# Binary cross entropy over two 8192 x 8192 matrices: chunks taken from the four quarters in turn, and the last chunk in four pieces

## The chip, the cores and the metric

One core of a Trainium2 chip. Times are device microseconds of one execution, medians of several runs. The granted clock was 1.0. A "span" is the profiled part of one execution, about 1.85 us shorter than its time.

## The reference

```python
# pred: uniform 0.01..0.99, target: 0 or 1; both (8192, 8192) float32
pred = np.clip(pred, 1e-7, 1 - 1e-7)
return -(target * np.log(pred) + (1 - target) * np.log(1 - pred))
```

Both inputs must be read and one output written: 3 x 268.4 MB = 805.3 MB. Since target is 0 or 1, the kernel takes one logarithm: -ln|pred + target - 1|.

## The kernel before

The matrices are flattened and cut into n = 64 chunks of 128 partitions x 8192. A ring of four slots holds pred as float32 (the result overwrites it) and target as bf16; the cast is done by the transfer. Chunk k's pred, target and result are 4.194 MB each in DRAM.

```python
def load(k):
    queue = nc.sync if k == 0 else nc.gpsimd
    queue.dma_start(out=slot(ring_p, k), in_=pred_c[k])
    nc.gpsimd.dma_start(out=slot(ring_t, k), in_=target_c[k])

def store(k, off=0, w=W):
    queue = nc.sync if k >= n - 2 else nc.gpsimd
    queue.dma_start(out=out_c[k, :, off : off + w], in_=slot(ring_p, k, off, w))

# clip(k):  DVE   p = min(max(p, eps), 1 - eps)      (L67)
# front(k): DVE   p = (t - 1) + p                    (L73)
#           ACT   p = Abs(p)                         (L76)
#           ACT   p = Ln(p)                          (L77)
# back(k):  DVE   p = -p                             (L81)
...
for k in range(1, n - 1):
    clip(k); front(k); back(k - 1); store(k - 1)
    if k >= 2 and k - 2 + SLOTS < n:
        load(k - 2 + SLOTS)
back(n - 2)
store(n - 2)

h, q = W // 2, W // 4              # the last chunk: 4096, 2048, 2048
clip(n - 1)
front(n - 1, 0, h)
front(n - 1, h, q)
back(n - 1, 0, h)
store(n - 1, 0, h)
front(n - 1, h + q, q)
back(n - 1, h, q)
back(n - 1, h + q, q)
store(n - 1, h, h)
```

(The four statements on one line stand on lines of their own in the kernel.)

## Time and profile before

| | before |
|---|---|
| time, median of 3 runs | 1871.18 us (1870.36 to 1873.4) |
| span of the profiled run | 1869.4 us |
| DVE, ACT busy | 60%, 48% of the span |
| DRAM traffic | 805.3 MB, 431 GB/s over the span |
| clip starts once settled | 29.04 to 29.05 us apart |

From the page of the kernel before: busy tenths of each engine in 40 equal slices of the span (9 is 90% or more), the mean of the 16 DMA engines, what they moved on the on-chip side (a target chunk counts half there, being cast to bf16), and the DRAM traffic.

```profile
DVE  4946564666656656566565665656656666566564
ACT  3643644536355364453544535445354463553645
DMA  9999999999999999999999999999999999999998
GB/s 325 337 377 352 351 376 344 376 353 350 381 344 373 358 347 385 344 368 364 346 384 346 361 370 344 382 350 355 375 345 378 353 351 381 345 372 358 347 385 330
HBM read 536.87 MB, written 268.44 MB: 431 GB/s over the span
```

The DMA row is full but for the last slice; no compute engine is. That is a kernel bound by transfers. How near to a ceiling it runs is read from the pace of a DVE instruction that waits for a load. From the timeline of the kernel before (start us, duration us, engine, line, operation, out<-in; in brackets the idle time before it and what ended it):

```profile
344.98 4.43 DVE L67 TENSOR_SCALAR ring_p<-ring_p 128x8192 f32<-128x8192 f32 x1 [6.26 <-DMA ring_p<-in_pred_dram]
375.27 4.43 DVE L67 TENSOR_SCALAR ring_p<-ring_p 128x8192 f32<-128x8192 f32 x1 [6.94 <-DMA ring_p<-in_pred_dram]
...
549.85 4.43 DVE L67 TENSOR_SCALAR ring_p<-ring_p 128x8192 f32<-128x8192 f32 x1 [6.31 <-DMA ring_p<-in_pred_dram]
578.89 4.43 DVE L67 TENSOR_SCALAR ring_p<-ring_p 128x8192 f32<-128x8192 f32 x1 [6.29 <-DMA ring_p<-in_pred_dram]
```

Early on two starts can be 30.29 us apart; later they are 29.04 us apart, one chunk for one chunk: 12.58 MB / 29.05 us = 433 GB/s. The trace also records every DMA packet: a 32 KB packet took 1213 ns at the median, and the 99th percentile was 1226 ns.

The tail, from the same timeline. "x3" on the SP line merges the last three stores: the third issue ends at 1836.16 + 26.10 = 1862.26.

```profile
1799.12 4.43 DVE L67 TENSOR_SCALAR ring_p<-ring_p 128x8192 f32<-128x8192 f32 x1 [6.25 <-DMA ring_p<-in_pred_dram]
1808.86 8.69 DVE L73 SCALAR_TENSOR_TENSOR ring_p<-ring_t,ring_p 128x8192 f32<-128x8192 bf16 x1 [5.31 <-DMA ring_t<-in_target_dram]
...
1831.70 4.43 DVE L81 TENSOR_SCALAR ring_p<-ring_p 128x8192 f32<-128x8192 f32 x1 [9.82 <-ACT ring_p L77]
1836.05 4.42 DVE L67 TENSOR_SCALAR ring_p<-ring_p 128x8192 f32<-128x8192 f32 x1
1836.16 26.10 SPq L63 DMA_DIRECT2D out_dram<-ring_p  x3
1840.50 6.63 DVE L73 SCALAR_TENSOR_TENSOR ring_p<-ring_t,ring_p 128x4096 f32<-128x4096 bf16 x2
...
1860.67 1.23 DVE L81 TENSOR_SCALAR ring_p<-ring_p 128x2048 f32<-128x2048 f32 x1 [2.78 <-ACT ring_p L77]
```

And the tail in windows of 2 us (start:end, length, busy time of DVE, ACT and POOL with instruction counts, granted clock, mean busy share of the 16 DMA engines, GB/s):

```profile
1850.00:1852.00 2.00, 0.00 (x0) 2.00 (x1) 0.00 (x0) 1.00 1.02 442
1852.00:1854.00 2.00, 1.74 (x1) 2.00 (x2) 0.00 (x0) 1.00 0.42 180
1854.00:1856.00 2.00, 2.00 (x2) 1.93 (x2) 0.00 (x0) 1.00 0.48 205
1856.00:1858.00 2.00, 1.89 (x2) 1.22 (x1) 0.00 (x0) 1.00 1.12 475
1858.00:1860.00 2.00, 0.00 (x0) 1.97 (x2) 0.00 (x0) 1.00 0.98 418
1860.00:1862.00 2.00, 1.23 (x1) 0.64 (x1) 0.00 (x0) 1.00 0.08 33
1862.00:1864.00 2.00, 0.00 (x0) 0.00 (x0) 0.00 (x0) 1.00 0.72 303
1864.00:1866.00 2.00, 0.00 (x0) 0.00 (x0) 0.00 (x0) 1.00 1.14 483
1866.00:1868.00 2.00, 0.00 (x0) 0.00 (x0) 0.00 (x0) 1.00 0.62 262
```

There are two holes, at 1852 to 1856 and 1860 to 1862.

### The profile page before, as it was taken

Reading aid. Unit: us, or ns where it says so; the run is one execution under the profiler, and the core shown is the slowest. Engines: PE = TensorE matmul, PEld = TensorE weight load, DVE = VectorE, ACT = ScalarE, POOL = GpSimd, SP = SyncE. Lnnn points to the kernel's source line nnn. Section 1 sums busy time; section 2 is a strip of 40 time slices with the busy share of each in tenths; the row PEclk is TensorE's granted clock in tenths of the full one; section 3 lists DMA queues with packets and bytes.
Section 4 is the critical chain, followed back from the end, with each engine's and each line's share of the span. In section 5 each row is a group of like instructions: output and inputs, shape, how many; then the busy total and the mean of one; then the engine's idle time right before and its main releaser. Section 6 shows DMA issues by size and latency. Waiting matters only on the chain.

```text
span 1869.4 us, 755 instructions
## 1 busy us (share of the span) xinstructions
DVE 1117.4 (60%) x197; ACT 902.2 (48%) x134; POOL 110.6 (6%) x193
## 2 busy tenths in 40 slices
DVE  4946564666656656566565665656656666566564
ACT  3643644536355364453544535445354463553645
POOL 0210000000000000000000000000000000000000
DMA  9999999999999999999999999999999999999998
GB/s 325 337 377 352 351 376 344 376 353 350 381 344 373 358 347 385 344 368 364 346 384 346 361 370 344 382 350 355 375 345 378 353 351 381 345 372 358 347 385 330
DMA packets 27797, 671.14 MB, mean 359 GB/s; under 512 B 3088, under 2 KB 3088, under 8 KB 3088
## 3 DMA queue, kind: packets, MB, share of 16 engines
q0 software_dynamic: 27216, 658.52, 98.8%
q1 hardware_dynamic: 576, 12.58, 1.6%
q14 instruction: 5, 0.04, 0.0%
HBM read 536.87 MB, written 268.44 MB: 431 GB/s over the span
## 4 chain that ended last, share of the span: by engine, by line
issue 86%; DMA 6%; POOL 5%; DVE 2%; ACT 1%; POOLq 0%; DVEq 0%; PEldq 0%
DMA ring_t<-in_target_dram 4%; DMA out_dram<-ring_p 2%; POOL ring_t L59 2%; POOL out_dram L63 2%; POOL ring_p L58 1%; DVE ring_p L73 1%; ACT ring_p L76 1%; ACT ring_p L77 1%; DVE ring_p L81 1%; DVE ring_p L67 0%; POOLq L58 0%; DVEq L73 0%; PEldq L136 0%; POOLq L63 0%
## 5 line engine op out<-in xcount | busy, mean ns | idle before, releaser
L76 ACT ACTIVATE ring_p<-ring_p 128x8192 f32<-128x8192 f32 (+1 forms) x66 | 450.4, 6824 | 955.6 <-DVE ring_p L73 955.6
L73 DVE SCALAR_TENSOR_TENSOR ring_p<-ring_t,ring_p 128x8192 f32<-128x8192 bf16 (+1 forms) x66 | 556.5, 8433 | 325.1 <-DMA ring_t<-in_target_dram 325.0
L67 DVE TENSOR_SCALAR ring_p<-ring_p 128x8192 f32<-128x8192 f32 x64 | 283.3, 4426 | 400.9 <-DMA ring_p<-in_pred_dram 400.9
L77 ACT ACTIVATE ring_p<-ring_p 128x8192 f32<-128x8192 f32 (+1 forms) x66 | 450.4, 6824 | 2.1
L81 DVE TENSOR_SCALAR ring_p<-ring_p 128x8192 f32<-128x8192 f32 (+1 forms) x66 | 283.1, 4290 | 17.7 <-ACT ring_p L77 17.7
L63 POOL DMA_DIRECT2D out_dram<-ring_p x62 | 40.8, 658 | 1692.7 <-DVE ring_p L81 1662.7
L58 POOL DMA_DIRECT2D ring_p<-in_pred_dram x63 | 36.1, 573 | 18.4 <-DMA out_dram<-ring_p 18.1
L59 POOL DMA_DIRECT2D ring_t<-in_target_dram x64 | 35.3, 552 | 0.8 <-PEq L136 0.8
L87 ACT ACT_TABLE_LOAD x1 | 1.3, 1283 | 0.7 <-PEq L125 0.7
L86 DVE MEMSET warm<- 1x8 f32 x1 | 0.1, 65 | 0.8 <-PEq L125 0.8
L87 ACT ACTIVATE warm<-warm 1x8 f32<-1x8 f32 x1 | 0.2, 207 | 0.0
L125 POOL MEMSET const-float32-0.0<- 128x1 f32 x1 | 0.1, 99 | 0.2 <-issue 0.2
L125 POOL MEMSET const-bfloat16-1.0<- 128x1 bf16 x1 | 0.1, 102 | 0.0
L125 POOL MEMSET const-float32-1.0<- 128x1 f32 x1 | 0.1, 99 | 0.0
L125 POOL MEMSET const-uint8-127<- 128x1 uint8 x1 | 0.1, 99 | 0.0
## 6 DMA issues: line engine op xcount, KB each, us to landing
ring_p<-in_pred_dram POOLq DMA_DIRECT2D x63, 4096.0 KB, 34.5
out_dram<-ring_p POOLq DMA_DIRECT2D x62, 4096.0 KB, 25.3
ring_t<-in_target_dram POOLq DMA_DIRECT2D x64, 2048.0 KB, 43.6
ring_p<-in_pred_dram SPq DMA_DIRECT2D x1, 4096.0 KB, 19.6
out_dram<-ring_p SPq DMA_DIRECT2D x1, 4096.0 KB, 21.1
out_dram<-ring_p SPq DMA_DIRECT2D x2, 2048.0 KB, 6.9
```

What stands on the lines that cost most here:

```text
L58: queue.dma_start(out=slot(ring_p, k), in_=pred_c[k])
L59: nc.gpsimd.dma_start(out=slot(ring_t, k), in_=target_c[k])
L63: queue.dma_start(out=out_c[k, :, off : off + w], in_=slot(ring_p, k, off, w))
L67: nc.vector.tensor_scalar(out=p, in0=p, scalar1=EPS, scalar2=1 - EPS, op0=Alu.max, op1=Alu.min)
L73: nc.vector.scalar_tensor_tensor(out=p, in0=t, scalar=1.0, in1=p, op0=Alu.subtract, op1=Alu.add)
L76: nc.scalar.activation(out=p, in_=p, func=Act.Abs)
L77: nc.scalar.activation(out=p, in_=p, func=Act.Ln)
L81: nc.vector.tensor_scalar(out=p, in0=p, scalar1=-1.0, scalar2=None, op0=Alu.mult)
L86: nc.vector.memset(warm, 1.0)
L87: nc.scalar.activation(out=warm, in_=warm, func=Act.Ln)
L125: nc = _bacc.Bacc("TRN2", target_bir_lowering=False, num_devices=1)
```

## The change: intent and diff

The order of chunks changes: each quarter of the matrices is 16 chunks, and the new walk visits quarters so that over the run every quarter's store comes behind a load of every other quarter. The sizes and the order of the transfers on their queues stay. In the tail, the last chunk's clip moves ahead of the multiply of the last but one, and its passes become four of 2048.

```diff
+QUARTERS = [0, 0, 1, 0, 2, 0, 3, 1, 1, 2, 1, 3, 2, 2, 3, 3]
+
+def walk(n):
+    taken, order = [0] * 4, []
+    assert n % 32 == 0
+    for i in range(n):
+        q = QUARTERS[i // 2 % 16]
+        order.append(q * (n // 4) + taken[q])
+        taken[q] += 1
...
-        queue.dma_start(out=slot(ring_p, k), in_=pred_c[k])
-        nc.gpsimd.dma_start(out=slot(ring_t, k), in_=target_c[k])
+        queue.dma_start(out=slot(ring_p, k), in_=pred_c[order[k]])
+        nc.gpsimd.dma_start(out=slot(ring_t, k), in_=target_c[order[k]])
...
-        queue.dma_start(out=out_c[k, :, off : off + w], in_=slot(ring_p, k, off, w))
+        queue.dma_start(out=out_c[order[k], :, off : off + w], in_=slot(ring_p, k, off, w))
...
+        clip(n - 1)
         back(n - 2)
         store(n - 2)
 
-        h, q = W // 2, W // 4
-        clip(n - 1)
-        front(n - 1, 0, h)
-        front(n - 1, h, q)
-        back(n - 1, 0, h)
-        store(n - 1, 0, h)
-        front(n - 1, h + q, q)
-        back(n - 1, h, q)
-        back(n - 1, h + q, q)
-        store(n - 1, h, h)
+        q = W // 4
+        front(n - 1, 0, q)
+        front(n - 1, q, q)
+        front(n - 1, 2 * q, q)
+        back(n - 1, 0, q)
+        back(n - 1, q, q)
+        store(n - 1, 0, 2 * q)
+        front(n - 1, 3 * q, q)
+        back(n - 1, 2 * q, q)
+        back(n - 1, 3 * q, q)
+        store(n - 1, 2 * q, 2 * q)
```

More of the change, by code (lines that the diff above doesn't have):

```diff
@@ L13 @@
 SLOTS = 4
+QUARTERS = [0, 0, 1, 0, 2, 0, 3, 1, 1, 2, 1, 3, 2, 2, 3, 3]
[6 more added lines that the diff above has]
+        taken[q] += 1
+    assert sorted(order) == list(range(n))
+    return order
 @with_exitstack
@@ L50 @@
     warm = pool.tile([1, 8], fp32, name="warm", tag="warm")
+    order = walk(n)
     def slot(ring, k, off=0, w=W):
```

## The prediction

> **What bounds the kernel now.** The transfers do. In the page's slices the DMA engines are at 9 tenths or more in 39 of 40; DVE is busy 60%, ACT 48%. In order of time, the clip (L67) starts every 29.04 to 29.05 us from 492 us on, and each chunk moves 3 x 4.194 MB on the HBM side: 12.58 MB / 29.05 us = 433 GB/s. The Trainium skill, "DMA: Bandwidth & Descriptors", section "Where 436 GB/s comes from", gives 435.2 GB/s as the ceiling of the data path; the trace agrees within 1%. In the packet records a 32 KB packet takes 1213 ns, load or store, and a target packet 1227 ns. So in steady state an engine's packet rate binds.
>
> **Where time is lost.**
> 1. The first quarter. Clip starts from chunk 4 to chunk 17 are 29.33 us apart on average: 13 x 0.28 = 3.6 us in all. By the packet records some target packets of chunks 4 to 15, and none later, take 1.5 to 1.8 us. These are the first quarter. To blame is the place (that part of target), a pair of places (store and load both in quarter 0), or the time since the start; one trace does not tell.
> 2. The tail. A table of 2 us windows shows the DMA half idle from 1852 to 1856 and nearly idle from 1860 to 1862.5, together about 4.5 us: the first half's store is issued about 1854.6, the second's at 1861.9, and the span ends 7.5 us later.
>
> **What the change does.** Bytes, transfers and issue order stay. Only DRAM offsets change, and the last chunk's passes: 4 x 2048 in place of 4096 + 2 x 2048, its clip before the multiply of n-2.
>
> Tail, worked out from durations in the trace: the last pred should land near 1828 (29.05 after the one before), so the clip fits into DVE's 9.8 us wait before L81. The last target lands near 1838, the first quarter's subtract (2.3 us) ends at 1840.2, then ACT runs without gaps: 4 x (1.92 + 1.92) = 15.5 us, to 1855.7; the last multiply takes 1.2 us. Stores are issued at about 1849.2 (before: 1854.6; the DMA still has work until 1853) and 1857.0 (before: 1861.9). The end is 7.5 us later: 1864.5. Gain 4.9 us, all critical.
>
> Order of quarters: nothing in the steady state, since packets already run at their floor. Of the 3.6 us it saves all or most if the pair (store 0, load 0) is at fault, which now occurs in 4 chunks of 64 in place of 16; nothing if the place is; it adds some if other pairs are bad. I count -0.5 us.
>
> **Prediction:** 1871.2 - 4.9 - 0.5, some **1865.5 us**, range 1861.5 to 1871.5. Faster by over 2%: 0.01; within 2%: 0.96; slower by over 2%: 0.03.
>
> **What the profile would show.** Right: clips still 29.05 us apart; 32 KB packets at 1213 ns; DMA windows full until about 1858; the last store issued near 1857, the first half's near 1849; ACT without gaps over the last four quarters; span near 1864. If place is at fault, slow target packets move with quarter 0's chunks through the whole run; if time, they stay in the first 450 us; if the pair, they nearly vanish.
>
> **What would make it wrong.** Pairs of quarters that slow packets throughout; a last target later than 1838; a second half's store that queues behind the first (then the tail gains only 2 us).

## The result and the profile after

| | before | after |
|---|---|---|
| time, median of 4 runs | 1871.44 us (1870.36 to 1873.4) | 1870.27 us (1869.64 to 1870.86) |
| span of the profiled run | 1869.4 us | 1867.8 us |
| ratio | | 0.9993, 95% interval 0.9975 to 1.001 |

A ratio is the mean time of one kernel's runs over that of the other's of the same rounds, so not quite the ratio of the medians. The time lies within the predicted range, but the gain is 1.2 us by medians, 1.6 us by spans, where I had counted 5.4 us.

The page of the kernel after: still full DMA slices, now in the last one too.

```profile
DMA  9999999999999999999999999999999999999999
GB/s 326 337 378 351 351 376 343 377 355 348 382 345 372 360 344 386 344 368 364 342 390 341 365 368 341 388 345 360 372 343 383 348 356 376 345 377 353 351 382 342
```

The clips in the timeline of the kernel after (its L83 is the clip, L89 the subtract, L97 the multiply): again an irregular early pace (30.10 us here), and the same settled one. The clip of chunk 17 (counted from 0) starts at 491.74; in the kernel before it started at 491.75.

```profile
316.41 4.43 DVE L83 TENSOR_SCALAR ring_p<-ring_p 128x8192 f32<-128x8192 f32 x1 [6.32 <-DMA ring_p<-in_pred_dram]
346.51 4.43 DVE L83 TENSOR_SCALAR ring_p<-ring_p 128x8192 f32<-128x8192 f32 x1 [6.26 <-DMA ring_p<-in_pred_dram]
...
491.74 4.43 DVE L83 TENSOR_SCALAR ring_p<-ring_p 128x8192 f32<-128x8192 f32 x1 [6.25 <-DMA ring_p<-in_pred_dram]
520.80 4.43 DVE L83 TENSOR_SCALAR ring_p<-ring_p 128x8192 f32<-128x8192 f32 x1 [6.32 <-DMA ring_p<-in_pred_dram]
```

The tail in the timeline of the kernel after:

```profile
1827.87 4.43 DVE L83 TENSOR_SCALAR ring_p<-ring_p 128x8192 f32<-128x8192 f32 x1 [6.32 <-DMA ring_p<-in_pred_dram]
1832.21 4.42 DVE L97 TENSOR_SCALAR ring_p<-ring_p 128x8192 f32<-128x8192 f32 x1
1836.65 19.97 SPq L79 DMA_DIRECT2D out_dram<-ring_p  x3
1837.61 6.70 DVE L89 SCALAR_TENSOR_TENSOR ring_p<-ring_t,ring_p 128x2048 f32<-128x2048 bf16 x3 [0.98 <-DMA ring_t<-in_target_dram]
...
1855.04 1.23 DVE L97 TENSOR_SCALAR ring_p<-ring_p 128x2048 f32<-128x2048 f32 x1 [2.52 <-ACT ring_p L93]
```

The compute side did what was predicted, and slightly better: the clip fits into the old wait at 1827.9, the subtract starts when the target lands at 1837.6, and the last issue ends at 1836.65 + 19.97 = 1856.62, against 1862.26 before. So the last store is issued 5.6 us earlier, and the span ends only 1.6 us earlier. The windows of the kernel after show the rest:

```profile
1852.00:1854.00 2.00, 0.53 (x1) 1.97 (x2) 0.00 (x0) 1.00 0.86 369
1854.00:1856.00 2.00, 0.96 (x1) 1.01 (x1) 0.00 (x0) 1.00 0.94 401
1856.00:1858.00 2.00, 0.27 (x1) 0.00 (x0) 0.00 (x0) 1.00 1.03 442
1858.00:1860.00 2.00, 0.00 (x0) 0.00 (x0) 0.00 (x0) 1.00 0.98 418
1860.00:1862.00 2.00, 0.00 (x0) 0.00 (x0) 0.00 (x0) 1.00 1.03 442
1862.00:1864.00 2.00, 0.00 (x0) 0.00 (x0) 0.00 (x0) 1.00 0.44 188
1864.00:1866.00 2.00, 0.00 (x0) 0.00 (x0) 0.00 (x0) 1.00 0.12 49
```

The holes are filled, as predicted. But the transfers do not stop together: a share of 0.44 and then 0.12 (0.12 x 16 is about two engines) is a queue that most engines have emptied and a few have not. The trace shows this directly. Each transfer leaves 16 landing records. That agrees with the Trainium skill, "DMA: Bandwidth & Descriptors", section "Why a DMA increments its semaphore by 16 and not by 1": on the path through GpSimd all 16 engines post an increment, and only the full 16 means that the data has landed. Of the transfer that lands nearest to each time I take the last landing minus the first, the **lag** of the last engine. Also counted are "slow" packets: target packets of over 1300 ns that start within 50 us of the time given:

```
                 before               after
time, us     lag, us  slow pkts   lag, us  slow pkts
   50          0.53      16         0.57      28
  150          0.70      27         0.99      25
  250          1.19      22         2.77      21
  350          2.37      10         4.08      11
  450          3.92       7         3.98       4
  550          3.92       0         4.00       0
 1050          3.94       0         4.02       0
 1750          4.25       0         4.01       0
```

The engines start about half a microsecond apart. During the first 450 us of these two runs some packets are slow and the lag grows; from then on all run at the same packet time and the lag hardly changes. (Other runs below do not come to rest at 450 us; batch 3 counts them.) The packet records do not name their engine, so that a slow packet leaves *its* engine behind is inferred. The sums fit it: in the kernel before, the slow target packets took 24.9 us in all beyond 1227 ns each, and at the last target the other 15 engines stood 20.5 us in all behind the first. My "3.6 us of the first quarter" is about this lag. (The prediction put the slow packets at chunks 4 to 15 and 1.5 to 1.8 us; the records show 16 of the 82 already in chunk 3, and durations from 1.30 to 1.95 us.) The lag also decides what a hole in the tail is worth, because the engine that is last has work while the others wait. The landings of the last three stores (first and last of the 16 engines, us):

```
                       before                 after
store of n-2       1852.98 .. 1857.22    1852.89 .. 1856.89
first half, n-1    1860.67 .. 1862.07    1857.75 .. 1861.76
second half, n-1   1868.03 .. 1868.23    1862.60 .. 1866.62
```

Before, the last engine landed the first half 4.84 us after the store of n-2, which is pure transfer (2.1 MB / 4.85 us = 433 GB/s), then took 6.17 us for the second half: it was idle for 1.3 us. The others had stopped earlier and waited longer; all 16 then started the second half together and landed within 0.2 us of each other. After, the last engine takes 4.87 and 4.85 us and never stops. It could gain 1.3 us, and did; the rest of the hole had belonged to engines that were ahead.

**Theory A.** Each engine has the same bytes to move, the end is set by the engine with the largest lag, and the tail can gain only what *that* engine idles: 1.3 us. The order of quarters is worth nothing in itself. **Rival Q**: the order of quarters brought (part of) the gain. **Rival B**, my prediction: the end follows the issue of the last store. And on the origin of the lag: **theory D** (engines that start in step disturb each other until they have come apart) against **rival T** (something belongs to the first half millisecond of an execution).

### The profile page after: what moved, and what is told of

Same layout as the page of the kernel before. It is cut to its first block, busy times and chain, and to the rows that moved or that the text cites. A ratio compares the mean times of both kernels' runs of the same rounds, so it can differ in the third digit from the quotient of the medians.

```text
span 1867.8 us, 759 instructions
## 1 busy us (share of the span) xinstructions
DVE 1117.6 (60%) x199; ACT 902.3 (48%) x136; POOL 110.5 (6%) x193
## 4 chain that ended last, share of the span: by engine, by line
issue 87%; DMA 6%; POOL 5%; DVE 1%; ACT 1%; POOLq 0%; DVEq 0%; PEldq 0%
DMA ring_t<-in_target_dram 4%; DMA out_dram<-ring_p 2%; POOL ring_t L75 2%; POOL out_dram L79 2%; POOL ring_p L74 1%; DVE ring_p L89 1%; ACT ring_p L93 0%; ACT ring_p L92 0%; DVE ring_p L97 0%; POOLq L74 0%; DVEq L89 0%; PEldq L154 0%; POOLq L79 0%
## 5 line engine op out<-in xcount | busy, mean ns | idle before, releaser
L89 DVE SCALAR_TENSOR_TENSOR ring_p<-ring_t,ring_p 128x8192 f32<-128x8192 bf16 (+1 forms) x67 | 556.6, 8309 | 326.6 <-DMA ring_t<-in_target_dram 326.6
L83 DVE TENSOR_SCALAR ring_p<-ring_p 128x8192 f32<-128x8192 f32 x64 | 283.3, 4427 | 406.3 <-DMA ring_p<-in_pred_dram 406.3
L97 DVE TENSOR_SCALAR ring_p<-ring_p 128x8192 f32<-128x8192 f32 (+1 forms) x67 | 283.3, 4229 | 5.0 <-ACT ring_p L93 5.0
```

The costliest lines, as they stand in the source:

```text
L83: nc.vector.tensor_scalar(out=p, in0=p, scalar1=EPS, scalar2=1 - EPS, op0=Alu.max, op1=Alu.min)
L89: nc.vector.scalar_tensor_tensor(out=p, in0=t, scalar=1.0, in1=p, op0=Alu.subtract, op1=Alu.add)
L97: nc.vector.tensor_scalar(out=p, in0=p, scalar1=-1.0, scalar2=None, op0=Alu.mult)
```

## The experiments

### Batch 1: the parts of the change, one at a time

Edits against the kernel before. e1_quarters is the order of chunks alone, e2_tail the whole tail alone (both are parts of the diff above). The two halves of the tail:

```diff
# e3_clip: the clip moved, old pieces
+        clip(n - 1)
         back(n - 2)
         store(n - 2)
         h, q = W // 2, W // 4
-        clip(n - 1)
# e4_pieces: the clip stays behind, four pieces
         back(n - 2)
         store(n - 2)
-        h, q = W // 2, W // 4
+        q = W // 4
         clip(n - 1)
...          (then the four pieces of the change)
```

> Only the order of quarters, with the old tail. Theory A (the steady state runs at an engine's packet rate; early slow packets come with the time since the start, not with addresses): ratio 1.000 within 0.0007, slow target packets (over 1300 ns) only in the first 450 us, clip starts 29.05 us apart after that, last store issued near 1861.9 as before. Rival (the order of quarters brought the measured gain, by taking apart stores and loads of one quarter): ratio near 0.9993 or lower, and fewer slow packets than the 102 of before.

> Only the new tail, chunks in the old order. Theory A: the whole gain is here, ratio 0.9991 to 0.9994 (1.2 to 1.6 us), last store issued near 1856.5 but landed near 1866.6, that is 29.1 us after the last target (3 stores of 4.194 MB at 433 GB/s) where before took 30.4. Rival (the order of quarters brought it): ratio 1.000 and an end as before.

> Only the clip of the last chunk moved ahead of the multiply of chunk n-2; the old pieces (4096, 2048, 2048). Theory A (the engine that is last after 450 us of slow packets runs without a stop to the end, so a last store issued before about 1861 gains no more by coming earlier): last store issued near 1858.3, yet the same end as with the whole new tail, 29.1 us after the last target, ratio as e2_tail. Theory B (my prediction: the end comes 7.5 us after the issue of the last store): about 2 us worse than e2_tail by issue time (1858.3 against 1856.4), so that of before's 1861.9 two thirds are gained.

> Only the four pieces; the clip of the last chunk stays behind the multiply of chunk n-2. Last store issued near 1859.4. Theory A: again the same end as e2_tail, 29.1 to 29.4 us after the last target, though the issue is 3 us later than there. Theory B: 3 us worse than e2_tail.

Measured, 5 rounds on one chip (9 runs of the kernel before: median 1872.67 us, 1871.29 to 1875.36):

| run | median us | range | ratio to before, 95% |
|---|---|---|---|
| e1_quarters | 1871.4 | 1870.36 to 1872.08 | 0.9991 (0.9979 to 1.0004) |
| e2_tail | 1870.51 | 1868.95 to 1871.11 | 0.9986 (0.9973 to 0.9998) |
| e3_clip | 1870.02 | 1869.18 to 1871.99 | 0.9986 (0.9973 to 0.9998) |
| e4_pieces | 1869.93 | 1869.37 to 1872.54 | 0.9984 (0.9971 to 0.9998) |

Times alone do not separate these, so read the traces. From the landing of the last target (its last engine) to the end of the issue of the last store, and to the landing of that store:

```
             last issue after target   landed after target   last two landings apart
before              24.45 us                30.42 us                6.17 us
e1_quarters         24.39                   30.38                   6.15
e2_tail             19.11                   29.11                   4.85
e3_clip             21.85                   29.09                   4.85
e4_pieces           21.66                   29.08                   4.84
after               19.11                   29.11                   4.85
```

The issue comes from the SP line of each timeline; that of e3_clip, for instance, which gives 1836.30 + 22.72 = 1859.02, less the target's 1837.17:

```profile
1836.30 22.72 SPq L63 DMA_DIRECT2D out_dram<-ring_p  x3
```

Rival B falls: e3_clip and e4_pieces issue 2.7 and 2.6 us later than e2_tail and end at the same distance. Either half of the tail's change alone brings the whole gain; the two do not add. All three end 29.1 us after the last target, which is the time that the three stores still to be moved take at 433 GB/s (3 x 4.194 MB / 433 GB/s = 29.06 us). As long as the last engine has these bytes to move, no order of the last chunk's passes can do better at this packet rate. In e3_clip the mechanism stands in its last store's landings: 14 engines within 0.2 us of the first, one 0.67 us behind, the last one 1.48 us behind. The 14 had stopped and waited for the issue; the last had not.

e1_quarters keeps before's tail to 0.04 us and its slow packets stay (93 of all sizes against 102). But one thing that Theory A expected of it failed: 15 of its 73 slow target packets start after 500 us, the last at 1107 us, and not "only in the first 450 us". By time the order of quarters is left undecided here: 0.9991 with an interval that holds 1. (That ratio is just outside the expected 1.000 within 0.0007, and e2_tail's 0.9986 just below its expected range; both intervals hold what was expected.)

### Batch 2: where the lag comes from, and whether it can be had for less

e5_drain is the kernel before with a drain: chunk 32 takes the slot of chunk 31, so that its loads wait for that chunk's store, and the loads of chunks 32 to 35 are issued only there.

```diff
# e5_drain, against the kernel before
+DRAIN = 32
-        c = k % SLOTS * W + off
+        c = (k - (k >= DRAIN)) % SLOTS * W + off
         for k in range(1, n - 1):
+            if k == DRAIN:
+                back(k - 1)
+                store(k - 1)
+                for j in range(k, k + SLOTS):
+                    load(j)
             clip(k)
             front(k)
-            back(k - 1)
-            store(k - 1)
-            if k >= 2 and k - 2 + SLOTS < n:
+            if k != DRAIN:
+                back(k - 1)
+                store(k - 1)
+            if k >= 2 and k - 2 + SLOTS < n and not DRAIN <= k - 2 + SLOTS < DRAIN + SLOTS:
                 load(k - 2 + SLOTS)
# e6_sp_pred, against the kernel after
-        queue = nc.sync if k == 0 else nc.gpsimd
+        queue = nc.sync
# e8_w4096, against e2_tail
-W = 8192
-SLOTS = 4
+W = 4096
+SLOTS = 6
# e7_nocast: e8_w4096, and
-    ring_t = pool.tile([P, SLOTS * W], bf16, ...)
+    ring_t = pool.tile([P, SLOTS * W], fp32, ...)
```

> The kernel before (old tail, old order) with one drain in the middle: chunk 32 takes the slot of chunk 31, so its loads wait for that chunk's store and all 16 engines fall idle and start again together. Theory D (engines that start in step disturb each other and come apart by it; each slow packet leaves its engine behind for good): the lag of the last engine behind the first falls from 3 to 7 us to under 1 us at the drain, then slow target packets come again, 30 to 100 of them, mostly in the 450 us after it, and the lag grows again to 3 to 7 us; periods after the drain 29.2 to 29.4 us at first. Rival T (something that belongs to the first half millisecond of an execution): no slow packets after the drain, lag stays under 1 us, periods 29.05 us. Either way the idle time of the drain itself costs some 11 us (estimate: 8 us for the passes behind the last store but one, 3 us to land and restart).

> The kernel after, with all pred loads issued from SP in place of GpSimd, so that each engine takes packets of pred and target in turn from two queues. If the slow packets come where all engines are in a target load at once, they get fewer and the lag of the last engine falls below 2 us: up to 3 us faster than after. If mixing does nothing for them: time as after within 1 us. If the mixed order delays pred so that the passes run late, a new wait shows and it is slower.

> Straight order, new tail, chunks of half the width in 6 slots, target loaded as float32, without the cast. If the cast is what slows packets: no target packets well above the median, lag of the last engine under 1 us to the end, 2 to 4 us less than e8_w4096. If any load does it: lag grows as in e8_w4096.

> The control of e7_nocast: the same chunks of half the width in 6 slots, target still cast to bf16 by the transfer. Expected: slow target packets in the first part, lag of the last engine 3 to 7 us, time within 3 us of e2_tail.

Measured on another chip (7 runs of the kernel before: median 1870.63 us, 1870.38 to 1871.6):

| run | median us | ratio to before, 95% | lag at the end of the loads |
|---|---|---|---|
| e5_drain | 1887.98 | 1.0092 (1.0072 to 1.0112) | 3.2 us |
| e6_sp_pred | 1872.53 | 1.0009 (0.9994 to 1.0024) | 4.0 us (target queue) |
| e7_nocast | 1882.66 | 1.0063 (1.0048 to 1.0078) | 5.8 us |
| e8_w4096 | 1879.33 | 1.0045 (1.0028 to 1.0062) | 5.4 us |

**e5_drain** settles D against T. Lag and slow target packets, counted as above:

```
time, us   lag, us   slow pkts
   50        0.38       21
  350        3.35        8
  550        4.26        3
  850        4.16        0
  950        0.17        0     <- just after the drain
 1050        0.58       52
 1150        1.92       30
 1250        2.53       14
 1350        3.22        7
 1450        3.26        0
 1750        3.14        0
```

The drain wipes out the lag, and the same history follows a second time in this one profiled run: slow packets for some 400 us, a growing lag, then rest. The clips show it in the timeline of e5_drain (L68 is its clip):

```profile
1057.69 4.43 DVE L68 TENSOR_SCALAR ring_p<-ring_p 128x8192 f32<-128x8192 f32 x1 [15.99 <-DMA ring_p<-in_pred_dram]
1086.98 4.43 DVE L68 TENSOR_SCALAR ring_p<-ring_p 128x8192 f32<-128x8192 f32 x1 [6.25 <-DMA ring_p<-in_pred_dram]
...
1204.80 4.43 DVE L68 TENSOR_SCALAR ring_p<-ring_p 128x8192 f32<-128x8192 f32 x1 [6.28 <-DMA ring_p<-in_pred_dram]
1234.08 4.43 DVE L68 TENSOR_SCALAR ring_p<-ring_p 128x8192 f32<-128x8192 f32 x1 [6.28 <-DMA ring_p<-in_pred_dram]
```

Six periods in 176.39 us are 29.40 us each, where the same run had 29.05 us before the drain (869.56 to 898.61, not shown). So the slow packets follow a restart of the transfers, not an address and not the first half millisecond of an execution; rival T falls. What it is in a restart stays open. That the engines disturb each other while in step was not measured by itself, and it does not explain all: in e4_pieces and f_both slow packets keep coming while the last engine is 3 to 8 us behind. The drain also issues four chunks of loads in one burst with no store between them, as the start does; no run separates the two. The drain cost some 17 us by medians. The packet records show all 16 engines idle for 5.2, 4.3 and 2.0 us there, 11.5 us in all, which is the idle time that I had estimated; the other 6 us were not pursued.

**e6_sp_pred** was a miss as a remedy. The packet records show the two queues taken in turn, some 16 packets of each. But the slow packets move to the 32 KB packets (113 of them over 1300 ns, and 8 target packets), the target queue has a lag of up to 7.7 us and 4.0 us at its last transfer, and the kernel is no faster than the one before; the kernel after was not in this batch.

**e7_nocast and e8_w4096** clear the cast: without it the lag grows to 5.8 us, with it to 5.4 us. My expectation that the run without a cast would stay under 1 us failed. Both are slower than the kernel before, for reasons that I did not pursue: e8_w4096 by 8.7 us, where I had expected it within 3 us of e2_tail, and e7_nocast is 3.3 us slower than its control, where I had expected 2 to 4 us less.

### Batch 3: the square, on a third chip

Kernel before, each half alone, both; no new edit.

> The kernel before itself, as one corner of a square with f_quarters, f_tail and f_both on one chip. Its ratio to before shows the noise: 1.000 within 0.0008. In its profile the last target should land near 1833.5 us plus the lag of the last engine, whatever that lag is this time (3 to 7 us), and the end 30.4 us later.

> e1_quarters again. Theory A: the order of quarters is worth nothing, mean time within 0.8 us of f_before and of before, end 30.4 us after the last target. Rival Q (the order lowers the lag that the engines pick up): about 1.5 us less than f_before, lag under 3.5 us in the profile.

> e2_tail again. Theory A: 1.3 us less than f_before within 0.8 us, end 29.1 us after the last target.

> The kernel after again. Theory A: the same as f_tail within 0.8 us. Rival Q: 1.5 us less than f_tail.

Measured, 5 rounds (9 further runs of the kernel before: median 1871.22 us, 1870.1 to 1874.75):

| run | median us | range | ratio to before, 95% |
|---|---|---|---|
| f_before | 1871.81 | 1870.34 to 1873.24 | 1.0003 (0.9989 to 1.0017) |
| f_quarters | 1870.52 | 1869.8 to 1872.5 | 0.9998 (0.9986 to 1.0011) |
| f_tail | 1869.29 | 1868.74 to 1870.79 | 0.9989 (0.9977 to 1.0002) |
| f_both | 1873.4 | 1871.88 to 1873.53 | 1.0008 (0.9995 to 1.002) |

f_quarters ran as Theory A had it, and with a lag of 5.2 us where rival Q needed less than 3.5 us. f_tail was 2.2 us faster than f_before by means, just outside the 1.3 us within 0.8 us that I had expected; its traced tail, 29.09 us, is as expected. f_both is the kernel after, and my expectation for it failed: all its five runs are slower than all five of f_tail. The trace says where it went, though not why. The windows of f_both near its end:

```profile
1860.00:1862.00 2.00, 0.09 (x1) 0.00 (x0) 0.00 (x0) 1.00 0.67 287
1862.00:1864.00 2.00, 0.00 (x0) 0.00 (x0) 0.00 (x0) 1.00 0.94 393
1864.00:1866.00 2.00, 0.00 (x0) 0.00 (x0) 0.00 (x0) 1.00 0.95 401
1866.00:1868.00 2.00, 0.00 (x0) 0.00 (x0) 0.00 (x0) 1.00 0.11 49
1868.00:1870.00 2.00, 0.00 (x0) 0.00 (x0) 0.00 (x0) 1.00 0.06 25
```

From 1866 to 1870 two engines, then one (0.06 x 16 is one engine) move the remaining bytes alone. Its lag was 7.94 us. Here are all profiled runs with chunks of 8192, without a drain and with the loads on one queue (in us):

```
run          lag   last target   target - lag   to last landing   time     time - lag - tail
before       4.21    1837.81       1833.60           30.42       1871.25       1836.62
f_before     3.41    1836.96       1833.55           30.36       1870.34       1836.57
e1_quarters  5.19    1838.69       1833.50           30.38       1872.08       1836.51
f_quarters   5.21    1838.50       1833.29           30.41       1871.91       1836.29
e2_tail      3.06    1836.84       1833.78           29.11       1868.95       1836.78
f_tail       3.85    1837.20       1833.35           29.09       1869.29       1836.35
e3_clip      3.65    1837.17       1833.52           29.09       1869.27       1836.53
e4_pieces    7.07    1840.44       1833.37           29.08       1872.54       1836.39
after        4.01    1837.51       1833.50           29.11       1869.64       1836.52
f_both       7.94    1841.34       1833.40           29.11       1873.45       1836.40
```

"Tail" in the last column is the column "to last landing". Times from 1868.95 to 1873.45 collapse to 1836.29 to 1836.78 us once two numbers are taken off: the lag, which the slow packets deal out, and the tail, which the code sets to 30.4 or 29.1 us. In these ten runs nothing else moves the time by more than 0.5 us. (Lag and tail together are the stretch from the last target's first landing to the end. So what the collapse shows is that the engine that is first gets there at the same time in every run, 1833.3 to 1833.8 us.)

The lag does not come to rest at 450 us in every run. From the landing of chunk 16's target, at about 472 us, to the last target:

```
run          lag at 472 us   lag at the end   slow target packets after 500 us
before            3.96            4.21                 0
f_before          3.44            3.41                 2
e1_quarters       4.46            5.19                15
f_quarters        3.64            5.21                21
e2_tail           2.68            3.06                 3
f_tail            3.38            3.85                 8
e3_clip           3.42            3.65                 2
e4_pieces         3.38            7.07                35
after             4.02            4.01                 0
f_both            5.67            7.94                37
```

The two largest lags, of e4_pieces and f_both, come from slow packets that went on, in f_both until 1804 us. Summed over a run, what slow target packets took beyond 1227 ns is alike in all ten, 17.7 to 25.3 us, and 21.7 and 23.6 us in these two. What differs is when it comes and how much of it the last engine gets.

What stays open is whether the order of quarters shifts the lag. The four profiled runs with it had 4.0, 5.2, 5.2 and 7.9 us, the six without it 3.1 to 4.2 and once 7.1 us (e4_pieces). Three of the four have 15 to 37 slow target packets after 500 us; of the six, five have 0 to 8 and e4_pieces has 35. The unprofiled runs don't decide it: the kernel after was 1.2 us faster than before on its first chip, and f_both 2.2 us slower (by medians) on another. f_both against f_tail suggests that an order can be worse on a given chip; nothing shows that it is better. I did not identify which engines fall behind.

## Why the prediction was right or wrong, point by point

- **"An engine's packet rate binds" in the steady state**: right. Settled clips are 29.05 us apart before, after, and in the part runs; 32 KB packets took 1213 ns at the median in both. New addresses changed neither.
- **Order of quarters, -0.5 us**: no gain of its own was shown; in one batch the kernel with it was slower than the tail alone. By its own test (slow packets that stay in the first 450 us mean "time"), place and pair fell at once: chunks 32 to 35 of the new walk lie in quarter 0 and no slow target packet came with them. The slow packets after 500 us in f_both fell on all four quarters too. But "time since the start" was not the cause either: e5_drain brings slow packets back with a restart, and in e4_pieces and f_both they never stopped at 450 us. That the kernel before had them in its first quarter alone was a coincidence of 16 chunks with some 450 us.
- **The compute side of the tail**: right. Target predicted at about 1838, seen at 1837.5; last store predicted at 1857.0, its issue ended at 1856.62; ACT without gaps; windows full.
- **The step that failed: "The end is 7.5 us later: 1864.5. Gain 4.9 us, all critical."** The 7.5 us from issue to end held only because before's engines had stopped and restarted together. After, the last store landed 10 us after its issue, on an engine 4.0 us behind the first. The term was mis-sized: 1.3 us measured by landings in place of 4.9 us. I had listed this as what would make it wrong ("a second half's store that queues behind the first (then the tail gains only 2 us)"), and the mean share of windows had hidden it: "about 4.5 us" of idle DMA was idle for the engines that were ahead.
- **The range** held by its width, not by the mechanism: its upper end, 1871.5 us, lies above the 1871.2 us of the kernel before, so it would have held with no gain at all. On the chip of f_both the median of the same kernel, 1873.4 us, lies outside it: I had taken the lag to be fixed, while over the ten runs it is 3 to 8 us.

## What to carry to other kernels

When a kernel is bound by transfers, its end is set by the slowest of the 16 DMA engines, and a mean busy share of 0.5 near the end must not be read as half the time to be gained: look at how far apart the landings of one transfer are. Issue the last stores before that engine runs dry; earlier than that gains nothing, and here one moved instruction was enough. Where a change is worth one microsecond in a run that varies by four, compare the traces' invariants (here, from the last load's landing to the end) and not the medians.

## What the Trainium skill lacked or had wrong

- "DMA: Bandwidth & Descriptors", section "Where 436 GB/s comes from": its ceiling of 435.2 GB/s agrees with the settled 433 GB/s of one core here, in bytes on the DRAM side. It is reckoned from the on-chip ports, and for the casting loads these are not what binds: a target packet brings 16 KB on chip in 1227 ns, 214 GB/s over 16 engines, and takes as long as a 32 KB packet without a cast (1213 ns). Its remark that for HBM to SBUF transfers the HBM side (about 358) binds does not hold for one core alone: 431 GB/s of DRAM traffic over the whole span; the same passage goes on with 425 GB/s measured for one load. "HBM Reference", section "Specifications (TRN2)", says it better: a core streaming alone measures about 425 GB/s; the runs here sustain slightly more.
- No page that I read says that the 16 engines, once started together, lose time to slow packets (in the kernels before and after, 16 KB target packets of up to 1.95 and 2.25 us in place of 1227 ns), all of it in the first 450 us there but about a third of it later in e4_pieces and f_both, and end 3 to 8 us apart; nor that a drain sets the lag to 0.2 us and that slow packets come again after it.
- "DMA: Bandwidth & Descriptors", section "Latency and other measured facts", says that engines 7 and 15 are usually slower and guesses at contention for descriptor rings. No run here shows which engines fall behind; settled, 32 KB packets take 1213 ns at the median and 1226 ns at the 99th percentile, and what differs is the lag picked up from slow packets, from 3.1 to 7.9 us between runs.
- No page that I read says that this lag explains nearly all of the spread between runs of a transfer-bound kernel: here 4.5 us of spread among ten profiled runs of its variants, 0.5 us when lag and tail are taken off.
